# Mixture-of-experts stage: residual parts of the weights two pieces per instruction, one-instruction results, and later transposes of the next rows

## The chip, the cores and the metric

One core of a Trainium2 chip runs the whole layer in one launch. The metric is the device time of that launch in microseconds (us); lower is better. The engines are TensorE (PE, with its weight loads as PEld), VectorE (DVE), ScalarE (ACT), GpSimd (POOL) and SyncE (SP, which only starts transfers here).

## The reference, cut to what matters

The layer is attention followed by a mixture of experts: 1024 tokens, width 1024, 32 experts, four experts per token. Only the experts are touched by the change. Cut, for the rows that an expert receives:

```python
hcat = xb @ w_in[e] + b_in[e]                       # 1024 -> 2048
x_glu = jnp.minimum(hcat[:, :D_FF], 7.0)
x_lin = jnp.clip(hcat[:, D_FF:], -7.0, 7.0)
act = x_glu * jax.nn.sigmoid(1.702 * x_glu) * (x_lin + 1)
y = act @ w_out[e] + b_out[e]                       # 1024 -> 1024
# y times the row's gate is added to the row's token
```

All in float32.

## The kernel before

The experts' stage (`stage_e`) goes through experts one by one, in an order that is written out by hand; the order of the calls is the order on every engine. Expert `e` first multiplies up to 128 gathered rows by `w_in[e]` into `H` (PSUM, four banks), in 16 **input pieces** `i` (`in_mm`): a piece is 128 rows by 1024 columns of the weights. After these, PE works on the 8 **output pieces** `k` of the expert before (`out_mm(e - 1, k)`), which multiply its activations by `w_out`. Between pieces stand other steps, at places that a few constants set: `COLS`, `KB`, `KAB`, `ACI`, `RI`, `LB`.

A float32 product is made of three fast ones (`mm3`, lines 87 to 89). The weight piece is split into a high part `wh` (ACT copies it into the type `F32R`, line 1131) and a low part `wl` (DVE subtracts `wh` from the raw weights, line 1132); the three products are high by high, low by high, high by low, for two halves of 512 columns, six matmuls a piece. `wh` and `wl` are rings of `NW` = 5 tiles. `split_ahead(1)` stands behind each piece and issues the split of the piece five places later, which has to wait until PE has finished the piece that frees its tile.

The steps that the change touches or moves past:

- `columns(e + 1, g)`, three groups g = 0, 1, 2: four transposes of the next expert's rows on PE (line 1119) into a buffer of the PSUM tag `r`, then an ACT copy (line 1122 or 1125) and, for g = 0 and 1, a DVE subtraction (line 1123, `xt`). They stand behind output pieces `COLS` = (1, 3, 4).
- `ring()`: the tag `r` has two buffers, used in turn by everything that asks: `L[e]` (two buffers, set to zero by ACT behind input piece 11), the three groups of `columns`, one blank buffer behind output piece `KB` = 5, and three groups of `act_cols` among the input pieces of the next round. Whoever asks waits until the last reader of the buffer two requests earlier is done.
- `act_a`, `act_l`, `act_b`: the activation. `act_a` (DVE lines 1195, 1197, ACT line 1196) and `act_l` (DVE lines 1204 and 1205 twice each, ACT line 1206) stand behind the input pieces. `act_l` reads the two buffers of `L[e]`.
- `left_in`, `left_out`: an expert's rows beyond 128, under a branch. Without such rows PE jumps over them.
- `result(e - 2)`: behind input piece 1, DVE scales the outputs by gate and modulation into `o` (line 1272, two halves) and `ol` (line 1276), and POOL adds them to the tokens with scattered transfers (lines 1278, 1283).

Of the kernel before, what the change touches and what calls it, by code (L numbers as in the profile page):

```python
# [9 lines left out]
F32 = mybir.dt.float32  # L10
F32R = mybir.dt.float32r
# [3 lines left out]
AF = mybir.ActivationFunctionType  # L15
OP = mybir.AluOpType
# [4 lines left out]
D = 1024  # L21
# [27 lines left out]
class K:  # L49
# [30 lines left out]
    def split(self, hi, lo, src):  # L80

        self.nc.scalar.activation(hi, src, AF.Copy)
        self.nc.vector.tensor_sub(lo, src, hi.bitcast(F32))
# [929 lines left out]
    def stage_e(self):  # L1013
        nc, I, tc = self.nc, self.I, self.tc
# [3 lines left out]
        with ExitStack() as ctx:  # L1018
            sp = self.pool("e1", ctx=ctx)
            ps = self.pool("eps", space=PSUM, ctx=ctx)  # L1020
            ctx.enter_context(tc.manual_schedule())
            RAW_IN, RAW_OUT, XG, XT, ACT, H, L, Y, HL = {}, {}, {}, {}, {}, {}, {}, {}, {}
            VAL = {}

            nrin = [len(self.first) - 2]
            NW = 5

            def rin():
                nrin[0] += 1
# [65 lines left out]
            def sel(e, q, n=128):  # L1095
                return self.selm[:, q, e:e + 1].to_broadcast([128, n])
# [28 lines left out]
                    nc.scalar.activation(xc, p3, AF.Copy)  # L1125
                    XG.pop(e)

            def split_w(src):
                h = sp.tile([128, 1024], F32R, name="wh", tag="wh", bufs=NW)
                l = sp.tile([128, 1024], F32R, name="wl", tag="wl", bufs=NW)  # L1130
                nc.scalar.activation(h, src, AF.Copy)  # L1131
                nc.vector.tensor_tensor(l, src, h.bitcast(F32), op=OP.subtract)  # L1132
                return h, l

            def in_split(e, i):
                k, h = divmod(i, 2)
                HL["in", e, i] = split_w(RAW_IN[e][k][:, 1024 * h:1024 * h + 1024])

            def out_split(e, k):
                HL["out", e, k] = split_w(RAW_OUT[e][k // 2][:, 1024 * (k % 2):1024 * (k % 2) + 1024])  # L1140

            def in_mm(e, i):
                k, h = divmod(i, 2)
# [13 lines left out]
            def beyond(e, unit):  # L1157

                with tc.If(VAL[e] > 128):
                    unit(0)  # L1160
                    with tc.If(VAL[e] > 160):
                        unit(1)
# [24 lines left out]
                beyond(e, unit)  # L1187

            A, AL = {}, {}
            COLS, KB, ACI, RI, LB, KAB = (1, 3, 4), 5, (3, 5, 7), 1, 11, 6  # L1190

            def act_a(e):
                gm = sp.tile([128, D], F32, name="ga", tag="ga", bufs=1)
# [40 lines left out]

            def out_mm(e, k):
                if k == 0:
                    Y[e] = [ps.tile([128, 512], F32, name="y", tag="y", bufs=2) for _ in range(2)]
                    for b in range(2):
                        nc.tensor.matmul(Y[e][b], sel(e, 1), self.bias[:, 512 + 512 * b:1024 + 512 * b],
                                         start=True, stop=False)  # L1240
                wh, wl = HL.pop(("out", e, k))
                ah, al, _ = ACT[e]
                for b in range(2):
                    c = slice(512 * b, 512 * b + 512)
                    self.mm3(Y[e][b], ah[:, k, :], al[:, k, :], wh[:, c], wl[:, c], False, k == 7)

            def left_out(e):
                ac = ACT[e][2]
                p = Y[e][2]

                def unit(u):
                    for j in range(4):
                        nc.tensor.matmul(p[32 * j:32 * j + 32, 256 * u:256 * u + 256],
                                         sel(e, 1, 32).bitcast(F32),
                                         self.bias[:, 512 + 256 * j:768 + 256 * j].bitcast(F32),
                                         start=True, stop=False, tile_position=(0, 32 * j))
                    for k in range(8):
                        jj, h = divmod(k, 2)
                        for j in range(4):
                            nc.tensor.matmul(p[32 * j:32 * j + 32, 256 * u:256 * u + 256],  # L1260
                                             ac[:, 2 * u + h, 32 * jj:32 * jj + 32],
                                             RAW_OUT[e][k // 2][:, 1024 * (k % 2) + 256 * j:1024 * (k % 2) + 256 * j + 256],
                                             start=False, stop=k == 7, tile_position=(0, 32 * j))

                beyond(e, unit)

            def result(e):
                y0, y1, yl = Y.pop(e)
                o = sp.tile([128, D], F32, name="o", tag="o", bufs=1)
                for b, y in enumerate((y0, y1)):  # L1270
                    c = slice(512 * b, 512 * b + 512)
                    nc.vector.scalar_tensor_tensor(o[:, c], y, self.gm[:, e:e + 1], self.gt2[:, c],  # L1272
                                                   op0=OP.mult, op1=OP.mult)
                ol = sp.tile([128, 2, 256], F32, name="ol", tag="ol", bufs=1)
                for u in range(2):
                    nc.vector.scalar_tensor_tensor(ol[:, u], yl[:, 256 * u:256 * u + 256], self.gl[:, u, e:e + 1],
                                                   self.gt2l, op0=OP.mult, op1=OP.mult)
                sc = [nc.gpsimd.indirect_dma_start(  # L1278
                    out=self.acc[:, :], out_offset=bass.IndirectOffsetOnAxis(ap=self.im[:, e:e + 1], axis=0),
                    in_=o, in_offset=None, compute_op=OP.add)]  # L1280
                for u in range(2):
                    nc.gpsimd.memset(spacer, 0.0)
                    i = nc.gpsimd.indirect_dma_start(  # L1283
                        out=self.acc.rearrange("t (j d) -> (t j) d", j=4),
                        out_offset=bass.IndirectOffsetOnAxis(ap=self.il[:, u, e:e + 1], axis=0),
                        in_=ol[:, u, :], in_offset=None, compute_op=OP.add)
                    for x in sc:
                        tc.declare_no_dep(i.ins, x.ins, reason="an expert's tokens are distinct, and so are the dummies")
                    sc.append(i)
# [18 lines left out]
            def split_ahead(used=0):  # L1308

                done[1] += used  # L1310
                while done[0] < min(len(seq), done[1] + NW):
                    kind, e, i = seq[done[0]]
                    if e not in (RAW_IN if kind == "in" else RAW_OUT):
                        break
                    (in_split if kind == "in" else out_split)(e, i)
                    done[0] += 1

            columns(0, 0)
# [2 lines left out]
            for e in range(NE + 1):  # L1321
                if 0 < e < NE - 1:
                    gather(e + 1)
                for i in range(16 if e < NE else 0):
                    in_mm(e, i)
                    if e > 0 or i < 13:
                        split_ahead(1)
                    else:
                        done[1] += 1
                    if i == RI and e > 1:  # L1330
                        result(e - 2)
                    if i in ACI and e > 0:
                        act_cols(e - 1, ACI.index(i))
                    if i == 0 and e == 0:
                        LLS = left_lists()
                    if i == 2 and e == 0:
                        left_lists2(*LLS)
                        gather_left(0)
                        load_out(0, range(2, 4), nc.gpsimd)
                    if i in (9, 10) and e == 0:  # L1340
                        columns(1, i - 9)
                    if i == 11 and e == 0:
                        columns(0, 2)
                        gather_left(1)
                    if i == LB:
                        L[e] = [blank(), blank()]
                if e == NE:
                    result(e - 2)
# [14 lines left out]
                for k in range(8 if e > 0 else 0):  # L1363
                    out_mm(e - 1, k)
                    split_ahead(1)
                    if e < NE:
                        if k in COLS and e + 1 < NE:
                            columns(e + 1, COLS.index(k))
                        if k == (KAB if e < NE - 1 else 3):
                            act_b(e)  # L1370
                        if e == NE - 1 and k in (5, 6, 7):
                            act_cols(e, (5, 6, 7).index(k))
                    if k == KB:
                        Y[e - 1].append(blank())
                if e == 0:
                    act_b(e)
                if e > 0:
                    left_out(e - 1)
                    if e < NE:
                        if e < NE - 1:  # L1380
                            load_out(e)
                        split_ahead()
# [168 lines left out]
```

## Time and profile before

| | |
|---|---|
| median of 3 runs | 2448.65 us (2445.6 to 2449.65) |
| the profiled execution | 2445.95 us |
| its span, first to last instruction | 2444.2 us |
| mean granted TensorE clock | 0.977 of full speed |
| PE, DVE, ACT busy | 93%, 79%, 62% of the span |

The profiled execution stands 2.7 us below the median of the runs. Its span leaves 1.75 us around it. The experts take about the last three fifths of the span, from 937 us on. In the traces a wait in brackets is the idle time of the engine ahead of an instruction, with the instruction that ended it; matmul ends are modelled, so a gap between matmuls is best read from start to start.

### The profile page before, as it was taken

Reading aid. Unit: us, or ns where it says so; the run is one execution under the profiler, and the core shown is the slowest. Engines: PE = TensorE matmul, PEld = TensorE weight load, DVE = VectorE, ACT = ScalarE, POOL = GpSimd, SP = SyncE. Lnnn points to the kernel's source line nnn. Section 1 sums busy time; section 2 is a strip of 40 time slices with the busy share of each in tenths; the row PEclk is TensorE's granted clock in tenths of the full one; section 3 lists DMA queues with packets and bytes.
Section 4 is the critical chain, followed back from the end, with each engine's and each line's share of the span. In section 5 each row is a group of like instructions: output and inputs, shape, how many; then the busy total and the mean of one; then the engine's idle time right before and its main releaser. Section 6 shows DMA issues by size and latency. Waiting matters only on the chain. (4 is left out here: it accounts for less than half of the span.)

```text
span 2444.2 us, 36800 instructions
## 1 busy us (share of the span) xinstructions
PE 2275.3 (93%) x13516; PEld 1760.8 (72%) x13516; DVE 1938.9 (79%) x3051; ACT 1505.0 (62%) x2285; POOL 549.3 (22%) x699
## 2 busy tenths in 40 slices
PE   6999999999999997989999999999999999999993
PEld 3787777787888775767667777767767777777762
DVE  5897087777998677988768898778878978887884
ACT  4321077777888324767656776666767766766762
POOL 2402100000344433122112222112212212222211
PEclk9999999999999997999999999999999999999996
DMA  7546141111110646889778898879779779787875
GB/s 266 182 142 198 48 141 36 35 27 44 30 24 18 231 162 241 326 339 330 263 265 334 306 350 316 292 266 370 279 279 384 285 296 355 281 321 299 311 272 173
DMA packets 133890, 557.00 MB, mean 228 GB/s; under 512 B 18720, under 2 KB 29632, under 8 KB 100880
## 3 DMA queue, kind: packets, MB, share of 16 engines
q1 hardware_dynamic: 103472, 476.21, 51.0%
q0 software_dynamic: 30176, 77.43, 11.4%
q8 instruction: 169, 2.77, 0.5%
q14 instruction: 73, 0.60, 0.1%
HBM read 495.04 MB, written 50.14 MB: 223 GB/s over the span
## 5 line engine op out<-in xcount | busy, mean ns | idle before, releaser
L1131 ACT ACTIVATE wh<-rin 128x1024 fp32r<-128x1024 f32 x520 | 550.3, 1060 | 251.4 <-PE H L89 218.8
L1132 DVE TENSOR_TENSOR wl<-rin,wh 128x1024 fp32r<-128x1024 f32 x520 | 619.4, 1219 | 102.2 <-ACT wh L1131 100.8
L87 PE MATMUL H<-wh,xt 128*128 128x512 f32 x1024 | 414.1, 404 | 0.6 <-issue 0.5
L88 PE MATMUL H<-wl,xt 128*128 128x512 f32 x1024 | 405.5, 396 | 0.6 <-DVE wl L1132 0.6
L89 PE MATMUL H<-wh,xt 128*128 128x512 f32 x1024 | 405.2, 396 | 0.0
L1132 DVE TENSOR_TENSOR wl<-rout,wh 128x1024 fp32r<-128x1024 f32 x248 | 296.5, 1222 | 88.4 <-ACT wh L1131 84.6
L1131 ACT ACTIVATE wh<-rout 128x1024 fp32r<-128x1024 f32 x248 | 256.7, 1054 | 47.1 <-PE H L89 27.2
L89 PEld LDWEIGHTS H<-wh,xt 128*128 128x128 f32 x1024 | 193.5, 189 | 45.7
L87 PEld LDWEIGHTS H<-wh,xt 128*128 128x128 f32 x1024 | 193.9, 189 | 43.5 <-issue 1.4
L88 PEld LDWEIGHTS H<-wl,xt 128*128 128x128 f32 x1024 | 194.0, 189 | 42.7 <-DVE wl L1132 1.0
L87 PE MATMUL y<-wh,at 128*128 128x512 f32 x512 | 210.8, 412 | 0.0
L88 PE MATMUL y<-wl,at 128*128 128x512 f32 x512 | 203.2, 397 | 0.5 <-DVE wl L1132 0.5
L89 PE MATMUL y<-wh,at 128*128 128x512 f32 x512 | 203.4, 397 | 0.0
L1060 POOL DMA_INDIRECT xg<-h2d,im x31 | 33.5, 1081 | 658.8 <-PE r L1119 658.2
L622 ACT ACTIVATE PT<-T 128x512 f32<-128x512 f32 (+1 forms) x256 | 140.8, 577 | 54.4 <-PE T L621 51.9
L1283 POOL DMA_INDIRECT acc<-ol,il x64 | 151.3, 2364 | 17.0 <-DVE wl L1132 15.2
L621 PE MATMUL T<-ident,P 128*128 128x128 f32 x960 | 149.6, 279 | 3.3 <-DVE m L547 2.7
L557 ACT ACTIVATE P<-S,m 128x1024 f32<-128x1024 f32 x128 | 142.9, 1117 | 13.8 <-DVE m L545 7.2
L1278 POOL DMA_INDIRECT acc<-o,im x32 | 51.7, 1615 | 409.0 <-DVE o L1272 377.0
L88 PE MATMUL g<-wl,hh 128*128 128x512 f32 (+1 forms) x368 | 138.0, 375 | 4.1 <-POOL wl L232 4.1
L87 PE MATMUL g<-wh,hh 128*128 128x512 f32 (+1 forms) x368 | 139.1, 378 | 1.1 <-ACT wh L231 0.6
L89 PE MATMUL g<-wh,xl 128*128 128x512 f32 (+1 forms) x368 | 137.3, 373 | 0.0
(338 smaller groups left out, 4376.4 us busy)
## 6 DMA issues: line engine op xcount, KB each, us to landing
rin<-in_w_in SPq DMA_DIRECT2D x252, 1024.0 KB
rout<-in_w_out SPq DMA_DIRECT2D x122, 1024.0 KB
ld<-in_w_ada SPq DMA_DIRECT2D x48, 512.0 KB
wr<-in_w_qkv SPq DMA_DIRECT2D x32, 256.0 KB
Q<-Q SPq DMA_DIRECT2D x32, 256.0 KB
xl<-in_x SPq DMA_DIRECT2D x8, 512.0 KB
xr<-in_x SPq DMA_DIRECT2D x8, 512.0 KB
acc<-x POOLq DMA_DIRECT2D x8, 512.0 KB, 5.5
```

The costliest lines, as they stand in the source:

```text
L87: nc.tensor.matmul(p, ah, bh, start=start, stop=False)
L88: nc.tensor.matmul(p, ah, bl, start=False, stop=False)
L89: nc.tensor.matmul(p, al, bh, start=False, stop=stop)
L557: nc.scalar.activation(parts[k][0], parts[k][1], AF.Exp, bias=m, scale=0.125, accum_out=l2[:, k:k + 1])
L621: nc.tensor.transpose(p[:, k, :], P[:, 128 * j:128 * j + 128], self.ident)
L622: nc.scalar.activation(PT[u - 1][:, 4 * g:4 * g + len(w), :], p[:, :len(w)], AF.Copy)
L1060: nc.gpsimd.indirect_dma_start(out=xg, out_offset=None, in_=self.h2d[:, :], in_offset=bass.IndirectOffsetOnAxis(ap=self.im[:, e:e + 1], ax ...
L1131: nc.scalar.activation(h, src, AF.Copy)
L1132: nc.vector.tensor_tensor(l, src, h.bitcast(F32), op=OP.subtract)
L1278: sc = [nc.gpsimd.indirect_dma_start(out=self.acc[:, :], out_offset=bass.IndirectOffsetOnAxis(ap=self.im[:, e:e + 1], axis=0), in_=o, in_o ...
L1283: i = nc.gpsimd.indirect_dma_start(out=self.acc.rearrange("t (j d) -> (t j) d", j=4), out_offset=bass.IndirectOffsetOnAxis(ap=self.il[:, u ...
```

## The change

It does five things, all in `stage_e`.

1. The rings have `NW` = 6 places instead of 5, and are one tile each, `WH` and `WL`, of six pieces.
2. A split is still one ACT instruction per piece. On DVE an even piece (first half of a raw weight tile) gets no instruction; the odd piece's instruction subtracts both halves, 2048 columns at once.
3. The groups of `columns` stand behind output pieces 3, 4, 5 instead of 1, 3, 4, and the blank buffer behind piece 6 instead of 5.
4. The output `y` is one PSUM tile of 1024 columns instead of two of 512, and `result` reads it with one DVE instruction.
5. The tiles `o` and `ol` take the buffers of `ln` and `lnl`, the linear half of the activation, instead of buffers of their own.

```diff
-            NW = 5
+            NW = 6
...
-            def split_w(src):
-                h = sp.tile([128, 1024], F32R, name="wh", tag="wh", bufs=NW)
-                l = sp.tile([128, 1024], F32R, name="wl", tag="wl", bufs=NW)
-                nc.scalar.activation(h, src, AF.Copy)
-                nc.vector.tensor_tensor(l, src, h.bitcast(F32), op=OP.subtract)
-                return h, l
...
+            WH = sp.tile([128, NW, 1024], F32R, name="wh")
+            WL = sp.tile([128, NW, 1024], F32R, name="wl")
+            npiece = [0]
+
+            def split(kind, e, i):
+                w = (RAW_IN if kind == "in" else RAW_OUT)[e][i // 2]
+                s, h = npiece[0] % NW, i % 2
+                npiece[0] += 1
+                nc.scalar.activation(WH[:, s], w[:, 1024 * h:1024 * h + 1024], AF.Copy)
+                if h:
+                    nc.vector.tensor_tensor(WL[:, s - 1:s + 1], w.rearrange("p (a b) -> p a b", a=2),
+                                            WH[:, s - 1:s + 1].bitcast(F32), op=OP.subtract)
+                HL[kind, e, i] = WH[:, s], WL[:, s]
...
-            COLS, KB, ACI, RI, LB, KAB = (1, 3, 4), 5, (3, 5, 7), 1, 11, 6
+            COLS, KB, ACI, RI, LB, KAB = (3, 4, 5), 6, (3, 5, 7), 1, 11, 6
...
-                    Y[e] = [ps.tile([128, 512], F32, name="y", tag="y", bufs=2) for _ in range(2)]
+                    y = ps.tile([128, 1024], F32, name="y", tag="y", bufs=1)
+                    Y[e] = [y[:, :512], y[:, 512:], y]
...
-                y0, y1, yl = Y.pop(e)
-                o = sp.tile([128, D], F32, name="o", tag="o", bufs=1)
-                for b, y in enumerate((y0, y1)):
-                    c = slice(512 * b, 512 * b + 512)
-                    nc.vector.scalar_tensor_tensor(o[:, c], y, self.gm[:, e:e + 1], self.gt2[:, c],
-                                                   op0=OP.mult, op1=OP.mult)
-                ol = sp.tile([128, 2, 256], F32, name="ol", tag="ol", bufs=1)
+                y, yl = Y.pop(e)[2:]
+                o = sp.tile([128, D], F32, name="o", tag="ln", bufs=1)
+                nc.vector.scalar_tensor_tensor(o, y, self.gm[:, e:e + 1], self.gt2, op0=OP.mult, op1=OP.mult)
+                ol = sp.tile([128, 2, 256], F32, name="ol", tag="lnl", bufs=1)
```

The first place is on DVE, behind `act_l` of the eleventh expert (e = 10), while PE works on the output pieces of the expert before. `rout` are raw tiles of `w_out`, `rin` those of the next expert's `w_in`, `xt` the subtraction of a group of `columns`. Before:

```order
L1205 TENSOR_SCALAR lnl_15609<-r_15454 128x256
L1132 TENSOR_TENSOR wl_15626<-rout_15285,wh_15625 128x1024
L1132 TENSOR_TENSOR wl_15636<-rout_15287,wh_15635 128x1024
L1123 TENSOR_TENSOR xt_15639<-r_15641,xt_15639 128x512
L1132 TENSOR_TENSOR wl_15655<-rout_15287,wh_15654 128x1024
L1132 TENSOR_TENSOR wl_15665<-rin_15592,wh_15664 128x1024
L1123 TENSOR_TENSOR xt_15639<-r_15668,xt_15639 128x512
```

And of the change:

```order
L1206 TENSOR_SCALAR lnl_14962<-r_14817 128x256
L1139 TENSOR_TENSOR wl_10241<-rout_14681,wh_10240 128x2048
L1139 TENSOR_TENSOR wl_10241<-rin_14945,wh_10240 128x2048
L1123 TENSOR_TENSOR xt_15001<-r_15003,xt_15001 128x512
L1123 TENSOR_TENSOR xt_15001<-r_15017,xt_15001 128x512
L1139 TENSOR_TENSOR wl_10241<-rin_14947,wh_10240 128x2048
```

Before, the first `xt` stands behind two splits of output pieces (5 and 6), and the second behind two more. Now both stand behind two instructions of 2048 columns: output pieces 6 and 7, and input pieces 0 and 1 of the next expert.

The second place is on ACT in the same stretch, from the last instruction of `act_l`. Before:

```order
L1206 ACTIVATE gal_15608<-gal_15608 128x512
L1131 ACTIVATE wh_15625<-rout_15285 128x1024
L1131 ACTIVATE wh_15635<-rout_15287 128x1024
L1122 ACTIVATE xt_15639<-r_15641 128x512
L1131 ACTIVATE wh_15654<-rout_15287 128x1024
L1131 ACTIVATE wh_15664<-rin_15592 128x1024
L1122 ACTIVATE xt_15639<-r_15668 128x512
```

And of the change:

```order
L1207 ACTIVATE gal_14961<-gal_14961 128x512
L1137 ACTIVATE wh_10240<-rout_14681 128x1024 x2
L1137 ACTIVATE wh_10240<-rin_14945 128x1024 x2
L1122 ACTIVATE xt_15001<-r_15003 128x512
L1137 ACTIVATE wh_10240<-rin_14947 128x1024
L1122 ACTIVATE xt_15001<-r_15017 128x512
```

Before, the copy of the first group (`xt`, line 1122) has two weight copies between it and `act_l`, now it has four, since the group stands two pieces later in the order.

## Rows read from the trace of the kernel before

**Rows 1.** The page, part 1: busy us (share of the span) and instructions.

```profile
PE 2275.3 (93%) x13516; PEld 1760.8 (72%) x13516; DVE 1938.9 (79%) x3051; ACT 1505.0 (62%) x2285; POOL 549.3 (22%) x699
```

**Rows 2.** Waits of PE, 500 to 2430 us: us in total, times, longest us.

```profile
PE r L1119 <- issue: 26.2, 15, 1.8
PE H L1148 <- PEq L1159: 9.3, 5, 3.2
...
PE H L88 <- DVE wl L1132: 0.6, 1, 0.6
```

**Rows 3.** Timeline, PE, eleventh expert: start, us, instruction, [idle before].

```profile
1413.43 0.39 PE L89 MATMUL y<-wh,at 128*128 128x512 f32 x1
...
1414.83 0.40 PE L89 MATMUL y<-wh,at 128*128 128x512 f32 x1
...
1416.97 0.63 PE L1119 MATMUL r<-ident,xg 128*128 128x128 f32 x4 [1.75 <-issue]
...
1417.36 0.47 PE L87 MATMUL y<-wh,at 128*128 128x512 f32 x1
```

**Rows 4.** Timeline, DVE, the same stretch and one expert later.

```profile
1410.24 3.70 DVE L1132 TENSOR_TENSOR wl<-rout,wh 128x1024 fp32r<-128x1024 f32 x3
1413.86 1.22 DVE L1195 TENSOR_SCALAR ga<-H 128x1024 f32<-128x1024 f32 x1
1415.00 1.21 DVE L1197 TENSOR_SCALAR ln<-H 128x1024 f32<-128x1024 f32 x1
...
1416.46 0.41 DVE L1205 TENSOR_SCALAR lnl<-r 128x256 f32<-128x256 f32 x1
...
1418.85 2.36 DVE L1132 TENSOR_TENSOR wl<-rout,wh 128x1024 fp32r<-128x1024 f32 x2 [1.32 <-ACT wh L1131]
1421.13 0.68 DVE L1123 TENSOR_TENSOR xt<-r,xt 128x512 fp32r<-128x512 f32 x1
...
1455.25 1.21 DVE L1197 TENSOR_SCALAR ln<-H 128x1024 f32<-128x1024 f32 x1
```

**Rows 5.** Timeline, ACT, the same stretch.

```profile
1411.63 1.06 ACT L1131 ACTIVATE wh<-rout 128x1024 fp32r<-128x1024 f32 x1 [0.34 <-PE H L89]
...
1417.24 0.63 ACT L1206 ACTIVATE gal<-gal 128x512 f32<-128x512 f32 x1 [1.07 <-DVE gal L1204]
1417.77 2.00 ACT L1131 ACTIVATE wh<-rout 128x1024 fp32r<-128x1024 f32 x2
1419.67 0.58 ACT L1122 ACTIVATE xt<-r 128x512 fp32r<-128x512 f32 x1
```

**Rows 6.** Groups by line, 500 to 2430 us: busy, mean ns.

```profile
L1132 DVE TENSOR_TENSOR wl<-rin,wh 128x1024 fp32r<-128x1024 f32 x520 | 619.4, 1219 | 102.2 <-ACT wh L1131 100.8
...
L1183 PE MATMUL r<-rin,xc 128*32 128x512 f32 x896 | 99.0, 592 | 0.0
...
L1212 DVE SCALAR_TENSOR_TENSOR gal<-lnl,gal 128x512 f32<-128x512 f32 x32 | 21.9, 683 | 0.0
```

**Rows 7.** Timeline, PE, around two longer idle stretches.

```profile
1100.73 1.19 PE L1148 MATMUL H<-bias,selm 128*128 128x512 f32 x2 [2.65 <-PEq L1159]
1101.72 0.63 PE L87 MATMUL H<-wh,xt 128*128 128x512 f32 x1
...
1684.32 1.19 PE L1239 MATMUL y<-bias,selm 128*128 128x512 f32 x2 [2.36 <-PEq L1159]
```

**Rows 8.** Windows, PE: us, PE busy (count), PEclk, DMA share, GB/s.

```profile
1100.00:1110.00 10.00, 9.27 (x36) 0.83 1.02 405
```

**Rows 9.** Timeline, PE and ACT, an expert with rows beyond 128.

```profile
1225.49 0.60 PE L1119 MATMUL r<-ident,xg 128*128 128x128 f32 x4
...
1228.95 1.06 ACT L1131 ACTIVATE wh<-rin 128x1024 fp32r<-128x1024 f32 x1 [0.30 <-PE y L89]
```

**Rows 10.** Timeline of POOL, and tile ol: its transfers' landing.

```profile
1439.44 2.54 POOL L1283 DMA_INDIRECT acc<-ol,il  x1 [0.26 <-DVE wl L1132]
...
DMA to landing us min/median/max: 4.2/9.5/11.1
```

More of the change, by code (lines that the diff above doesn't have):

```diff
@@ L1126, in columns @@
                     XG.pop(e)
-            def split_w(src):
-                h = sp.tile([128, 1024], F32R, name="wh", tag="wh", bufs=NW)
-                l = sp.tile([128, 1024], F32R, name="wl", tag="wl", bufs=NW)
-                nc.scalar.activation(h, src, AF.Copy)
-                nc.vector.tensor_tensor(l, src, h.bitcast(F32), op=OP.subtract)
-                return h, l
[L1135 to L1140, printed above, removed]
+            WH = sp.tile([128, NW, 1024], F32R, name="wh")
[10 more added lines that the diff above has]
+                HL[kind, e, i] = WH[:, s], WL[:, s]
             def in_mm(e, i):
@@ L1248, in left_out @@
                 ac = ACT[e][2]
-                p = Y[e][2]
+                p = Y[e][3]
                 def unit(u):
@@ L1314, in split_ahead @@
                         break
-                    (in_split if kind == "in" else out_split)(e, i)
+                    split(kind, e, i)
                     done[0] += 1
```

## The prediction

> **What bounds the kernel now.** I read the busy shares first: PE 93%, DVE 79%, ACT 62% [rows 1]. PE is nearly full, so the question is what PE waits for in the experts' stage. The view of PE's waits answers: for weights it waited once, 0.6 us; its largest wait is ahead of the transposes of line 1119, 26.2 us in 15 waits of up to 1.8 us, ended by nothing that the profile names [rows 2]. The timeline of the eleventh expert shows one: the last matmul of output piece 1 starts at 1414.83, the next could follow 0.23 later (six matmuls take 1413.43 to 1414.83, 1.40 us a piece), but the transposes start at 1416.97, so 1.91 us are lost [rows 3]. On DVE the first buffer of `L` gets its last reader, line 1205, from 1416.46 to 1416.87, 0.10 us before PE goes on [rows 4]. So the first group waits for its PSUM buffer, which `act_l` holds. This happens where PE jumps over `left_in`: line 1183's 896 records are 14 groups of 64 [rows 6], and the timeline gives two of these to one expert, so 13 experts have rows beyond 128. The first expert and the last don't have the step in this form; 17 of the other 30 experts jump. In two of the 17 a slow jump on PE had already used up the wait.
>
> **The change part by part.** *Moving the first group* to output piece 3 gives PE two more pieces, 2.80 us, before it asks for that buffer. Against that stands a later DVE, and then the third group. I lay out the eleventh expert anew.
>
> DVE. With six places, the split that waits for the last input piece is that of output piece 5 instead of 4; ACT still makes it at 1411.63 to 1412.69 [rows 5]. Behind it DVE now does 2048 columns. Its price isn't in the trace: 512 columns take 0.683 us and 1024 take 1.219 [rows 6], 0.536 for 512 more, so 2048 take 0.683 + 3 x 0.536 = 2.29 us. Two back to back, from 1418.85 to the next start at 1421.13, take 1.14 each, 0.08 under their duration [rows 4], so the pair holds DVE 2.21 us. The lower bound for the price is 2.0 (no fixed part, 2 x 1.0), the upper 2.44 (no saving at all). The pair ends its hold at 1412.74 + 2.21 = 1414.95, where `act_a` began at 1413.86 before [rows 4]: everything of the activation comes 1.09 us later. The first buffer is free at 1416.87 + 1.09 = 1417.96, and the group may start at 1418.07.
>
> PE. Piece 3 ends at 1415.06 + 2.80 = 1417.86. It waits 0.2 us instead of 1.91: the old wait is nearly gone. The group takes 0.39 [rows 3], piece 4 1.40, the second group 0.39, piece 5 1.40: PE reaches the third group at about 1421.65.
>
> ACT. Its `act_l` instruction started at 1417.24 and the next weight copy at 1417.77; two copies took until 1419.67, 0.95 each [rows 5]. Now 1.09 later: copies of output pieces 6 and 7 and of input pieces 0 and 1 at 1418.86, 1419.81, 1420.76 and 1421.71, all with free places by then, and only then the copy of the first group, 1422.66 to 1423.24.
>
> DVE again. The pair of output pieces 6 and 7 can start when the second copy ends, 1420.9, and holds DVE until 1423.1; the pair of input pieces 0 and 1 until 1425.3; then the first group's subtraction, 0.68 [rows 4], ends at 1426.0. That subtraction is the last reader of the buffer that the third group asks for, since the tag has two. So PE waits from 1421.65 to about 1426.05, **4.4 us**. Before, the subtraction ended at 1421.13 + 0.68 = 1421.81 [rows 4], about when PE got there. The wait moved from the first group to the third and grew: 4.4 + 0.2 - 1.91 = 2.7 us.
>
> For the 17: new waits 17 x 4.6 = 78 us; removed 15 x 1.91 = 29 us; net **+50**. Three pairs stand in this chain, so with a price of 2.0 or 2.44 it ends 0.9 earlier or 0.45 later: +35 to +58.
>
> *Experts with rows beyond 128* (13). There `act_l` is done before output piece 0 ends, and ACT waits for PE's pieces (0.30 us ahead of a copy) [rows 9]; the chain starts from PE. Group 1 came at 1225.49, when piece 1 ended [rows 9]. Piece 3 now ends 2.8 later, 1228.3, and frees the place of input piece 1: ACT copies it from 1228.55 to 1229.6, the pair runs until 1231.9, the subtraction until 1232.6. PE is at the third group after piece 3 + 0.39 + 1.40 + 0.39 + 1.40 = 1231.9. It waits 0.7; the later blank buffer may add 0.1 ahead of `left_out`. 13 x 0.8 = **+10** (bounds 0 and 15).
>
> *Start and end.* The first `wl` of the stage needs two copies and a pair instead of one of each: 1.06 + 2.29 - 1.22, 2.1 us. With the last expert's `act_b` behind pairs I take **+3** (bounds 0 and 8).
>
> *TensorE's clock.* After an idle stretch of 2.65 us matmuls take 0.63 instead of 0.40 us [rows 3, 7]; the window's mean granted clock is 0.83 [rows 8], that is 3.4 of 10 us at 1.2 instead of 2.4 GHz, 1.7 us of work lost. The stretch of 2.36 us shows the same matmuls of 1.19 [rows 7]; the 15 waits of 1.75 don't [rows 3]. A wait of 4.4 us is longer than any of these, so I expect falls. How much of the slow stretch lies inside the wait itself isn't seen: 0 to 1.7 us for each of 17. I take 1.2, nearer to the upper row: **+20** (0 to 29).
>
> *Parts at nothing.* A pair saves DVE 2 x 1.219 - 2.29 = 0.15 us, twelve times an expert, and `result` saves some too. DVE isn't what PE waits for outside this place: PE waited 0.6 us for a `wl` [rows 2], and DVE itself waited 102.2 us ahead of line 1132, nearly all for ACT [rows 6]. With a pair done some 3.5 us after the second copy starts and six places of 1.40 us, weights stay ahead. `o` and `ol` in the buffers of `ln` and `lnl` add waits of DVE for the scattered transfers, ahead of `act_a` and `act_l`, with the whole chain above queued behind. The last transfer was issued at 1439.44 and lands within 11.1 us, by 1450.5; line 1197 comes at 1455.25 [rows 4, 10]. Both move about a microsecond; 4 us of cover remain. Without it each microsecond would be paid by up to 30 experts. The transfers of weights wait for branches that PE passes, and a slower PE gives them more room. POOL's gathers wait for later transposes, but fetch rows a whole expert ahead (some 40 us).
>
> The Trainium skill, Perfetto Trace Analysis, section Optimizing Scalar/DVE Operations, has two rules here. Larger operations can raise throughput if the engine is saturated; by that the twelve pairs would give 30 x 12 x 0.15 = 54 us. But where an engine isn't saturated and still makes others idle, smaller instructions, which finish sooner, may help; by that the pairs give nothing and the chain above stays. DVE's waits for ACT say that the second applies.
>
> **The sum.** 50 + 10 + 3 + 20 = +83 us. On the profiled execution's 2445.95 that is 2529; on the median of the runs, 2448.65, it is **2531**.
>
> **The rivals.**
> - *The wait is there but the clock holds.* For it: the falls of rows 7 followed branches, none a buffer. Against: both stretches of rows 7 are shorter than this wait, and the clock fell. 2448.65 + 63 = 2512.
> - *The third group hardly waits: faster.* This is the change doing what its places suggest: the first buffer freed in time, and no new wait. It would give 17 x 0.2 - 29 = -26, with the start 2426. It decides at the third group: the first group's subtraction must end by 1421.65, 4.4 us sooner than laid out, which is just the two pairs (2 x 2.21) that the order puts ahead of it. An engine that took the subtraction ahead of them would do it; in all rows of DVE that I read, instructions run in the order of the program, and the copy on ACT alone, at 1422.66, is too late.
> - *DVE bounds after all*: then its 54 us less of work show in the time, 2395. Against: it stood idle for ACT [rows 6] and PE hardly for it [rows 2]. This is the first of the skill's two rules above.
> - *The wait is there but short*, 1 to 2.5 us, if ACT and DVE make up more of their delay than my lay-out gives: net 17 x (1.75 + 0.2) - 29 + 13 = +17, about 2466, and no clock falls.
> - *The scattered transfers come too late for `ln`*: on top of the sum 2 us in each of 30 experts would give 2591. It needs landings of 15 us, none above 11.1 is seen [rows 10].
>
> **How the numbers follow.** Forecast with clock falls 0.60, clock holding 0.20, short wait 0.09, no wait 0.07, DVE as the bound 0.01, late transfers 0.03. The likeliest case alone spans 2501 (+35, 0, 0, +17) to 2550 (+58, +15, +8, +20). For 8 in 10 the range takes in the clock's holding, with its low end at 2448.65 + 35 = 2484, and the upper end of the forecast: 2482 to 2552. Measurements of this kernel differ by up to 0.17% within three runs, so 0.2% (5 us) is about what can be told from no change. Faster 0.08; same 0.02, a part of the short wait; slower 0.90.
>
> **What would show it.** Right: in PE's waits the third group (transposes of `xgl`) waits some 4.4 us in 17 experts, ended by the subtraction of `xt`; waits of 1.75 us ahead of the first group fall to a few tenths; the pair takes 2.29 us; the mean granted clock falls below 0.977, with some 3.4 us at the lower level behind such waits; PE's total waits grow by about 60 us. Wrong: no idle time ahead of the `xgl` transposes, or the subtraction of the first group before the pair of input pieces 0 and 1 in time; then the gain of about 25 us would stand.

## The result and the profile after

| | before | changed |
|---|---|---|
| median of 4 runs each | 2447.12 us (2444.24 to 2449.65) | 2521.49 us (2518.6 to 2525.74) |
| ratio, 95% interval | | 1.0306 (1.0286 to 1.0326) |
| the profiled execution / its span | 2445.95 / 2444.2 us | 2520.61 / 2518.8 us |
| mean granted TensorE clock | 0.977 | 0.961 |

The change makes the kernel 74.4 us slower; the spans of the two profiled executions differ by 74.6. The forecast was 2531 (+83), range 2482 to 2552.

First the busy times on the page (part 1, busy us, share and instructions), beside [rows 1]:

```profile
PE 2299.8 (91%) x13516; PEld 1782.6 (71%) x13516; DVE 1901.4 (75%) x2635; ACT 1506.7 (60%) x2285; POOL 590.9 (23%) x699
```

DVE has 416 instructions and 37.5 us less to do, and nothing comes of it. PE runs the same 13516 instructions and is busy 24.5 us longer: the same matmuls took longer, and the granted clock fell from 0.977 to 0.961. The other 50 us are idle time. PE's waits, 500 to 2510 us (us in total, times, longest us), beside [rows 2]:

```profile
PE r L1119 <- DVE xt L1123: 74.7, 31, 4.1
PE H L1149 <- PEq L1160: 9.2, 4, 3.8
PE r L1227 <- DVE ga L1212: 6.5, 2, 6.0
...
PE H L88 <- DVE wl L1139: 2.5, 1, 2.5
```

The groups by line split line 1119 into the first two groups (`xg`) and the third (`xgl`); the last part of a row is the idle time ahead. The changed kernel:

```profile
L1119 PE MATMUL r<-ident,xg 128*128 128x128 f32 x256 | 39.5, 278 | 1.8 <-PE y L89 0.9 <-issue 0.3
...
L1119 PE MATMUL r<-ident,xgl 128*128 128x128 f32 x128 | 26.4, 341 | 78.0 <-DVE xt L1123 74.7 <-DVE lnl L1206 3.3
```

And the same two rows of the kernel before:

```profile
L1119 PE MATMUL r<-ident,xg 128*128 128x128 f32 x256 | 39.6, 279 | 26.8 <-issue 26.2 <-PE y L89 0.3 <-DVE gmain L854 0.3
...
L1119 PE MATMUL r<-ident,xgl 128*128 128x128 f32 x128 | 19.6, 276 | 3.3 <-DVE lnl L1205 3.3
```

The wait did not go away; it moved from the first group (26.8 to 1.8 us) to the third (3.3 to 78.0 us). The eleventh expert shows how, in the timeline of PE (start, us, instruction, [idle before]):

```profile
1436.91 0.39 PE L89 MATMUL y<-wh,at 128*128 128x512 f32 x1
1437.37 0.63 PE L1119 MATMUL r<-ident,xg 128*128 128x128 f32 x4
...
1440.83 0.40 PE L89 MATMUL y<-wh,at 128*128 128x512 f32 x1
1445.34 1.11 PE L1119 MATMUL r<-ident,xgl 128*128 128x128 f32 x4 [4.12 <-DVE xt L1123]
1446.11 0.77 PE L87 MATMUL y<-wh,at 128*128 128x512 f32 x1
1446.68 0.63 PE L88 MATMUL y<-wl,at 128*128 128x512 f32 x1
```

of DVE:

```profile
1436.85 0.42 DVE L1206 TENSOR_SCALAR lnl<-r 128x256 f32<-128x256 f32 x1
...
1440.19 2.29 DVE L1139 TENSOR_TENSOR wl<-rout,wh 128x2048 fp32r<-128x2048 f32 x1 [2.26 <-ACT wh L1137]
1442.40 2.28 DVE L1139 TENSOR_TENSOR wl<-rin,wh 128x2048 fp32r<-128x2048 f32 x1
1444.60 1.28 DVE L1123 TENSOR_TENSOR xt<-r,xt 128x512 fp32r<-128x512 f32 x2
```

and of ACT:

```profile
1438.17 1.99 ACT L1137 ACTIVATE wh<-rout 128x1024 fp32r<-128x1024 f32 x2
1440.06 1.99 ACT L1137 ACTIVATE wh<-rin 128x1024 fp32r<-128x1024 f32 x2
1441.96 0.58 ACT L1122 ACTIVATE xt<-r 128x512 fp32r<-128x512 f32 x1
```

The first group follows piece 3 after 0.46 us from start to start, 0.23 more than from one matmul to the next, where 1.91 us were lost before [rows 3]. Its copy on ACT ends at 1442.54, but its subtraction on DVE starts only at 1444.60, behind the two pairs that stand ahead of it in the order, and PE waits for it from 1441.06 to 1445.34, 4.28 us from start to start. Behind it matmuls start 0.43 us apart instead of 0.23. Windows of 5 us behind this wait and behind one that began at 1726 us (us, PE busy (count), PEclk, DMA share, GB/s):

```profile
1445.30:1450.30 5.00, 4.96 (x14) 0.50 1.03 419
1729.10:1734.10 5.00, 4.99 (x20) 0.66 1.02 421
```

0.50 is the lower level throughout; in the second window a part of the time is at the full clock. The timeline has 17 such waits, 15 of them of 4.06 to 4.13 us and two (from 1726 and 2256 us) of 3.1, where a slow jump over a branch stood ahead. Slow matmuls follow all 17. The other 14 of the 31 waits in the row above are of 0.48 us each: 13 in the experts with rows beyond 128, and one at 964 us, early in the stage.

### The profile page after: what moved, and what is told of

Same layout as the page of the kernel before. It is cut to its first block, busy times and chain, and to the rows that moved or that the text cites. A ratio compares the mean times of both kernels' runs of the same rounds, so it can differ in the third digit from the quotient of the medians.

```text
span 2518.8 us, 36232 instructions
## 1 busy us (share of the span) xinstructions
PE 2299.8 (91%) x13516; PEld 1782.6 (71%) x13516; DVE 1901.4 (75%) x2635; ACT 1506.7 (60%) x2285; POOL 590.9 (23%) x699
## 3 DMA queue, kind: packets, MB, share of 16 engines
q1 hardware_dynamic: 103472, 476.21, 49.7%
## 5 line engine op out<-in xcount | busy, mean ns | idle before, releaser
L1139 DVE TENSOR_TENSOR wl<-rin,wh 128x2048 fp32r<-128x2048 f32 x260 | 594.3, 2287 | 182.9 <-ACT wh L1137 182.8
L1139 DVE TENSOR_TENSOR wl<-rout,wh 128x2048 fp32r<-128x2048 f32 x124 | 284.3, 2293 | 130.1 <-ACT wh L1137 130.1
L87 PE MATMUL y<-wh,at 128*128 128x512 f32 x512 | 222.0, 434 | 0.0
L88 PE MATMUL y<-wl,at 128*128 128x512 f32 x512 | 210.9, 412 | 0.0
L89 PE MATMUL y<-wh,at 128*128 128x512 f32 x512 | 210.8, 412 | 0.0
L1060 POOL DMA_INDIRECT xg<-h2d,im x31 | 43.4, 1399 | 636.4 <-PE r L1119 635.8
L1068 POOL DMA_INDIRECT xgl<-h2d,il x64 | 125.1, 1955 | 131.5 <-PE r L1119 101.1
```

The source lines that it names most:

```text
L87: nc.tensor.matmul(p, ah, bh, start=start, stop=False)
L88: nc.tensor.matmul(p, ah, bl, start=False, stop=False)
L89: nc.tensor.matmul(p, al, bh, start=False, stop=stop)
L1060: nc.gpsimd.indirect_dma_start(out=xg, out_offset=None, in_=self.h2d[:, :], in_offset=bass.IndirectOffsetOnAxis(ap=self.im[:, e:e + 1], ax ...
L1068: nc.gpsimd.indirect_dma_start(out=xl[:, u, :], out_offset=None, in_=self.h2d.rearrange("t (j d) -> (t j) d", j=4), in_offset=bass.Indirec ...
L1139: nc.vector.tensor_tensor(WL[:, s - 1:s + 1], w.rearrange("p (a b) -> p a b", a=2), WH[:, s - 1:s + 1].bitcast(F32), op=OP.subtract)
```

## The experiments

The theory after the result: in an expert whose branch is jumped, the third group has to wait for the first group's PSUM buffer, whose last reader DVE takes behind two pairs of weight subtractions; the lower clock comes on top. Rivals: the later places alone or the longer instructions alone explain it; shared buffers or the ring tiles cost something; the longer busy time is not the idle time's doing. All were timed against the kernel before on the same chip. "Groups 1, 2" and "group 3" are PE's idle us ahead of their transposes, including 3.3 us ahead of one transpose near 970 us in every kernel.

| kernel | median us | ratio to before | groups 1, 2 | group 3 |
|---|---|---|---|---|
| before | 2447 to 2449 | 1 | 26.8 | 3.3 |
| changed | 2521.49 | 1.0306 (1.0286 to 1.0326) | 1.8 | 78.0 |
| e1_places | 2470.72 | 1.0091 (1.0060 to 1.0122) | 0.3 | 43.7 |
| e2_pairs | 2480.68 | 1.0143 (1.0112 to 1.0175) | 49.8 | 7.4 |
| e3_rest | 2446.97 | 0.9999 (0.9989 to 1.0009) | 30.8 | 3.3 |
| e4_order | 2465.32 | 1.0076 (1.0051 to 1.0100) | 2.2 | 32.6 |
| e5_bank | 2451.92 | 1.0014 (1.0004 to 1.0023) | 1.8 | 3.8 |
| e6_fill | 2499.81 | 1.0214 (1.0199 to 1.0230) | 2.2 | 12.9 |
| e9_places_234 | 2475.12 | 1.0111 (1.0091 to 1.0130) | 5.5 | 37.0 |
| e7_third_apart | 2430.77 | 0.9927 (0.9914 to 0.9941) | 5.0 | 3.3 |
| e8_all_apart | 2547.39 | 1.0395 (1.0380 to 1.0409) | 93.1 | 3.6 |
| e10_order_old | 2442.17 | 0.9974 (0.9962 to 0.9986) | 5.0 | 3.3 |

### The change taken apart: places, pairs, the rest

**e1_places**: the kernel before with the new places only.

```diff
-            COLS, KB, ACI, RI, LB, KAB = (1, 3, 4), 5, (3, 5, 7), 1, 11, 6
+            COLS, KB, ACI, RI, LB, KAB = (3, 4, 5), 6, (3, 5, 7), 1, 11, 6
```

> The kernel before with only the places changed: groups of transposes behind output pieces 3, 4, 5, blank buffer behind 6; five places, one subtraction per piece. Theory (the first group's subtraction is late, and the third group waits for its PSUM buffer): the activation is not delayed, so the first group does not wait; four copies and four subtractions of 1.14 us stand ahead of the first group's subtraction, which ends near 1424.1 in the eleventh expert's time while PE is there at 1421.45: a wait of about 2.7 us in 17 experts, 46 against 29 removed, +17 us, and some falls of the clock, in all +17 to +40. Rival (only the 2048-column instructions hurt, the places are good): the 29 us are gained, -25 us.

Measured +24 us. In PE's waits the same wait has appeared, shorter:

```profile
PE r L1119 <- DVE xt L1123: 40.4, 17, 2.5
```

The places alone move the wait to the third group; they give no gain.

**e2_pairs**: the changed kernel with the places of before, so the pairs and all the rest, but not the move.

```diff
-            COLS, KB, ACI, RI, LB, KAB = (3, 4, 5), 6, (3, 5, 7), 1, 11, 6
+            COLS, KB, ACI, RI, LB, KAB = (1, 3, 4), 5, (3, 5, 7), 1, 11, 6
```

> The changed kernel with the old places 1, 3, 4 and 5; pairs, six places, one-instruction results and shared buffers stay. Theory: the pair of output pieces 4 and 5 makes the activation 1.09 us later, so the first group waits 3.0 instead of 1.9 us in 17 experts, and the third 0.8: 65 against 29 before, +36 us, and falls of the clock after 3.0 us, in all +35 to +60. Rival (the new places alone make the loss, pairs save DVE work): 0 to -10 us.

Measured +34 us. The wait stays ahead of the first group and grows from 1.75 to about 3 us, since the pair delays the activation that frees the buffer. In the eleventh expert `act_a` on DVE starts 3.30 us after the start of ACT's last weight copy ahead of it, in the kernel before 2.23; so it comes 1.07 us later:

```profile
PE r L1119 <- DVE lnl L1206: 52.8, 18, 3.3
```

**e3_rest**: the changed kernel with the old places and one subtraction of 1024 columns per piece; the ring tiles with six places, the one-instruction result and the shared buffers stay.

```diff
-                if h:
-                    nc.vector.tensor_tensor(WL[:, s - 1:s + 1], w.rearrange("p (a b) -> p a b", a=2),
-                                            WH[:, s - 1:s + 1].bitcast(F32), op=OP.subtract)
+                nc.vector.tensor_tensor(WL[:, s], w[:, 1024 * h:1024 * h + 1024], WH[:, s].bitcast(F32), op=OP.subtract)
...
-            COLS, KB, ACI, RI, LB, KAB = (3, 4, 5), 6, (3, 5, 7), 1, 11, 6
+            COLS, KB, ACI, RI, LB, KAB = (1, 3, 4), 5, (3, 5, 7), 1, 11, 6
```

> The changed kernel with the old places and one subtraction of 1024 columns per piece: what is left are six places in one tile, one-instruction results, and o and ol in the buffers of ln and lnl. Theory: nothing of this is on the path, within 5 us of before, waits of 1.75 us ahead of the first group as before. Rival (the shared buffers make the activation wait for the scattered transfers, or the one-tile ring adds waits): a good part of the 74 us, +20 or more.

Measured 2446.97 us, ratio 0.9999 (0.9989 to 1.0009): these parts together cost and give nothing that can be measured. So the loss is the places' and the pairs': 24 and 34 us alone, 74 together, more than their sum of 58.

### The order, the buffer, the clock

**e4_order**: the changed kernel, but a group of `columns` is asked for ahead of `split_ahead(1)` behind the same piece, so one split fewer stands ahead of each copy and subtraction.

```diff
                     out_mm(e - 1, k)
+                    if e < NE and k in COLS and e + 1 < NE:
+                        columns(e + 1, COLS.index(k))
                     split_ahead(1)
                     if e < NE:
-                        if k in COLS and e + 1 < NE:
-                            columns(e + 1, COLS.index(k))
```

> The changed kernel with each group of transposes ahead of the split that follows the same output piece, not behind it. Theory: on ACT three copies instead of four, on DVE one pair instead of two stand ahead of the first group's subtraction, which then ends near 1423.8; PE is at the third group at 1421.65, so the wait falls from 4.3 to about 2.2 us, is gone in the 13 experts with rows beyond 128, and the clock falls hardly or not: 17 x 2.4 - 29 + 3, +15 us, at most +30. Rival (weights come late behind the long instructions, whatever stands in the order): near the changed kernel, +60 to +75.

Measured +18 us instead of the changed kernel's +74. The third group's wait falls from 4.12 to 1.92 us; the difference of 2.20 is what one pair holds DVE (starts at 1440.19, 1442.40 and 1444.60 above). Slow matmuls still follow 10 of the 15 waits, where hardly a fall of the clock was expected.

```profile
PE r L1119 <- DVE xt L1123: 29.3, 16, 1.9
```

So the pairs that stand ahead of the subtraction in the order make the wait: with one of the two gone from there, 56 of the 74 us are gone.

**e5_bank**: the changed kernel, but the third group doesn't ask the ring; it is written into the fourth bank of the next expert's `H`, which the activation has freed by then.

```diff
-                p = ring()
+                if g == 2 and e > 1:
+                    H[e] = ps.tile([128, 2048], F32, name="H", tag="H", bufs=1)
+                    p = H[e][:, 1536:2048]
+                else:
+                    p = ring()
...
-                if i == 0:
+                if i == 0 and e not in H:
```

> The changed kernel with one difference: the third group of transposes writes into the fourth PSUM bank of the next expert's H, which is free by then, and no longer asks for a buffer of the tag r. DVE and ACT keep their order and are as late as before. Theory (the wait is for the buffer): the waits of 4.1 us ahead of the third group are gone. What is late next is the low part of output piece 6, which the pair delivers at about 1423.2 in the eleventh expert's time, while PE asks at 1422.3: 1 us in 17 experts; the buffers of the tag come round one request earlier and may cost 1 to 2 us in some others. In all -5 to +25 us against before, no falls of the clock there. Rival (PE would wait anyway, for low parts that come as late as the subtraction): PE waits some 4 us at output piece 6 instead, near +74.

Measured +2.6 us. With all subtractions still behind the pairs, the wait ahead of the third group is gone but for the two experts that still use the ring, and some 72 us of the 74 with it. By line, as above:

```profile
L1123 PE MATMUL H<-ident,xgl 128*128 128x128 f32 x120 | 18.0, 272 | 0.0
L1123 PE MATMUL r<-ident,xgl 128*128 128x128 f32 x8 | 1.3, 283 | 3.8 <-DVE lnl L1210 3.3 <-DVE xt L1127 0.5
```

What is late next are smaller things:

```profile
PE r L1259 <- ACT r L1104: 12.0, 12, 1.6
PE y L88 <- DVE wl L1143: 9.7, 15, 0.7
```

The first is `left_out`, which asks for the ring in the experts with rows beyond 128; the second are weights that the pairs give later.

**e6_fill**: the changed kernel with 17 more matmuls ahead of the third group in the 17 experts that jump. They write a bank of the next expert's `H`, which is written anew later, so they change no output.

```diff
-                if i == 0:
+                if i == 0 and e not in H:
...
+                        if k == COLS[2] and e in (1, 2, 3, 4, 8, 9, 10, 11, 14, 16, 18, 20, 21, 24, 25, 27, 29):
+                            H[e + 1] = ps.tile([128, 2048], F32, name="H", tag="H", bufs=1)
+                            for _ in range(17):
+                                nc.tensor.matmul(H[e + 1][:, :512], sel(e, 1), self.bias[:, 512:1024],
+                                                 start=True, stop=True)
```

> The changed kernel, in which PE fills its long wait: in the 17 experts that jump over left_in, 17 extra matmuls (bias by selection, 0.23 us each, 4.0 us in all) into the next expert's H, which is written anew later, stand ahead of the third group. The chain on ACT and DVE is the same, so the third group starts when it did. Theory (20 of the 74 us are matmuls at 1.2 GHz behind the waits): PE stays busy, the clock does not fall there, some 15 to 25 us less than the changed kernel, about +52 against before. Rival (the clock's falls lie inside the waits and cost nothing, all 74 us are waits): as the changed kernel, +74, or more by what the extra matmuls overrun.

The fill takes the place of the idle time, and the third group comes 4.28 us late as before:

```profile
1438.45 0.40 PE L89 MATMUL y<-wh,at 128*128 128x512 f32 x1
1438.68 4.09 PE L1369 MATMUL H<-bias,selm 128*128 128x512 f32 x17
1442.96 0.66 PE L1119 MATMUL r<-ident,xgl 128*128 128x128 f32 x4 [0.19 <-DVE xt L1123]
1443.38 0.48 PE L87 MATMUL y<-wh,at 128*128 128x512 f32 x1
```

The granted clock of the stage (windows as above), in the changed kernel:

```profile
1000.00:2430.00 1430.00, 1325.58 (x7237) 0.97 0.80 298
```

and with the fill:

```profile
1000.00:2410.00 1410.00, 1365.88 (x7542) 1.00 0.81 301
```

The time is 2499.81 us, 1.0214 (1.0199 to 1.0230). PE does 289 matmuls more, and yet the kernel is faster than the changed one by 1.0306 - 1.0214 = 0.0092, some 22 us (by the two intervals 16 to 29), which is the clock's part. The timelines agree: from 937 us on, the matmuls of `mm3` that take 0.58 us or more number 31 before, 142 in the changed kernel and 32 with the fill. 120 of the 142 stand behind the 17 waits; at 0.43 instead of 0.23 us from start to start they cost 24 us. The remaining 50 us stay although PE isn't idle there: they are the lateness itself.

### Could the idea of the change pay?

**e7_third_apart**: the kernel before, with the edit of e5_bank (shown there) and the groups behind pieces 2, 3 and 4.

```diff
...
-            COLS, KB, ACI, RI, LB, KAB = (1, 3, 4), 5, (3, 5, 7), 1, 11, 6
+            COLS, KB, ACI, RI, LB, KAB = (2, 3, 4), 4, (3, 5, 7), 1, 11, 6
```

> A version for both: the kernel before (five places, 1024-column subtractions) with the third group in the fourth bank of the next expert's H, groups behind output pieces 2, 3, 4, blank buffer behind 4. Theory: PE reaches the first group at 1416.46 instead of 1415.06, its buffer is free at 1416.97, so 0.5 instead of 1.91 us in 17 experts, and no other wait takes its place, since only two groups ask the tag for buffers: 15 x 1.4 us, about -20, -12 to -25. Rival (the ring of buffers is needed by others too, the wait moves on to the activation's transposes): 0 to -8.

Measured 2430.77 us, 18.6 below the kernel before and faster than both. None of the waits for the subtraction is left:

```profile
PE r L1123 <- PE y L89: 4.6, 13, 0.4
```

The Trainium skill, Perfetto Trace Analysis, section Optimization Strategy, says that the same gap, repeated on the engine that should be full, can mean that SBUF or PSUM lacks room for the next tile. The traces agree: 15 equal waits of 1.75 us before, and with one bank more and the new places 13 of at most 0.4 us.

**e9_places_234**: the kernel before with those places, but all three groups in the ring.

```diff
-            COLS, KB, ACI, RI, LB, KAB = (1, 3, 4), 5, (3, 5, 7), 1, 11, 6
+            COLS, KB, ACI, RI, LB, KAB = (2, 3, 4), 4, (3, 5, 7), 1, 11, 6
```

> The kernel before with the places 2, 3, 4 and the blank buffer behind 4, all groups in the tag r: the version with the third group apart without its bank. Theory: the first group waits 0.5 us; three copies and three subtractions stand ahead of the first group's subtraction, which ends near 1422.95 in the eleventh expert's time, while PE asks for the third group's buffer at 1420.55: 2.4 us in 17 experts, 17 x 2.9 - 29 = +20 us, with falls of the clock up to +35. Rival (the gain with the third group apart came from the places, not from the bank): -12 to -20 us.

Measured +27 us, with 33.7 us of waits ahead of the third group. The gain of e7_third_apart needs the bank.

**e8_all_apart**: as e7_third_apart, but all three groups in banks 2 to 4 of the next `H`.

```diff
-                p = ring()
+                if e > 1:
+                    if g == 0:
+                        H[e] = ps.tile([128, 2048], F32, name="H", tag="H", bufs=1)
+                    p = H[e][:, 512 + 512 * g:1024 + 512 * g]
+                else:
+                    p = ring()
...
```

> As the one with the third group apart, but all three groups write into the second to fourth banks of the next expert's H, so none asks the tag r. Theory: the first group waits for act_a alone, which reads H until 1416.2, before PE is there at 1416.46: no wait is left, 15 x 1.75 us, about -24, -15 to -28; the activation's transposes may wait for the reader of the blank buffer where rows beyond 128 are, 1 us in some. Rival (the two buffers of the tag come round sooner and the waits move to the activation's transposes in most experts): -10 or less.

Measured 2547.39 us, 1.0395 (1.0380 to 1.0409): +98 where a gain was expected. Now the second group waits for the subtraction of the first, in all 30 experts, although they use different banks (4.3 to 4.6 us in 17 of them, 1.2 in 13):

```profile
PE H L1124 <- DVE xt L1128: 92.8, 30, 4.5
```

The program waits on DVE between two groups of the same tile `H`. Why it holds that wait between banks stays open. The miss fits the theory in so far as the same subtraction, awaited one group earlier, makes PE wait longer: 4.5 us, against 2.2 in e9_places_234.

**e10_order_old**: the kernel before with the order of e4_order (shown there) and the groups behind 2, 4 and 5.

```diff
-            COLS, KB, ACI, RI, LB, KAB = (1, 3, 4), 5, (3, 5, 7), 1, 11, 6
+            COLS, KB, ACI, RI, LB, KAB = (2, 4, 5), 5, (3, 5, 7), 1, 11, 6
...
```

> The kernel before with the groups behind output pieces 2, 4, 5, each ahead of the split that follows the same piece; no other buffer. Theory: the first group waits 0.5 us; its subtraction stands behind two subtractions as in the kernel before and ends at 1421.8, while PE asks for the third buffer at 1421.95: no wait. 15 x 1.4 us, -12 to -21. Rival (any later place delays the first group's subtraction past the third group): 0 to +20.

Measured 2442.17 us, 0.9974 (0.9962 to 0.9986): a gain of 5.6 us, less than expected. The waits ahead of the groups are gone as meant (4.6 us in 14 small ones), but in its profile more is lost elsewhere: behind the branches 32.8 us against 25.6 before, and in two waits ended by nothing that the profile names 4.2 us against 0.5 in one:

```profile
PE H L1148 <- PEq L1159: 14.9, 6, 4.1
PE H L1148 <- PEq L1161: 7.4, 11, 2.8
PE y L1239 <- PEq L1161: 5.5, 12, 0.5
PE y L1239 <- PEq L1159: 5.0, 5, 2.1
PE r L1119 <- issue: 4.6, 14, 0.4
PE H L87 <- issue: 4.2, 2, 2.3
```

In the profiles of the other ten kernels the rows behind branches add up to 21 to 27 us. The profiled execution, 2445.45 us, is also one of the longer of the 12, which go from 2434.77 to 2449.38. Whether the removed wait comes back there, or these waits merely vary from execution to execution, was not settled.

## Why the prediction came out as it did

The mechanism was right; the sum, 83 against 74, was 9 us too high, chiefly by the waits of the groups.

- **The pair.** Priced at 2.29 us with a hold of 2.21; measured 2.29 and 2.20. The lower bound of 2.0 was looser than its rows: four times 0.536 is 2.14 without a fixed part. The long instruction delays what stands behind it, as laid out (1.07 us in e2_pairs, where 1.09 was forecast): 34 us alone. DVE's saving was put too high, at 54 us: two subtractions back to back take 2.36 us and not 2 x 1.22, so a pair saves 0.07 there, and with the results DVE has 37.5 us less to do. The Trainium skill, Perfetto Trace Analysis, section Optimizing Scalar/DVE Operations, has the rule on smaller instructions that the prediction weighed against the one on larger ones. It is the one that held: with less to do on DVE e2_pairs loses 34 us, and e3_rest without the pairs loses nothing.
- **First group.** 0.2 us left of 1.91; measured 0.23 from start to start.
- **Third group.** 4.4 us; measured 4.28. Order and durations of ACT and DVE came as laid out; e4_order and e5_bank show that the pairs and the buffer make it. But two of the 17 waits were shorter, 3.1 us of idle time: a slow jump had already used up part, as in two of the old waits, and the prediction counted those for the old wait alone. From start to start the 17 experts lose 45 us more, where 50 were forecast.
- **Experts with rows beyond 128.** 0.8 us each; measured 0.65 from start to start (0.48 of idle time), and 1.3 us in all ahead of `left_out`, 0.1 each. This term held.
- **Idle time ahead of the groups together.** The rows by line give (1.8 + 78.0) - (26.8 + 3.3) = 49.7 us, where the sum had 50 + 10 = 60. About half of the difference is the measure: the sum went from start to start, and by that the two terms come to 45 + 10 = 55. The other half is the two shorter waits and 0.12 us less in each of the 15.
- **Start and end.** 3 us; at the start PE waited 2.5 us for the first `wl` instead of 0.6 [rows 2], so 1.9 (2.1 forecast). The kernel before has a second wait for a `wl`, 0.5 us near its end, where the prediction speaks of one; it is gone. At the end line 1227 waited 6.0 us for the last expert's `act_b`. The same wait was 3.2 us before, so 2.8 where about 1 was meant. Together some 5 us.
- **Clock.** 20 us; by e6_fill 22. The value between the ends of 0 and 29 was chosen and not worked out, so that it came this near is luck in part. The reason given, that a wait longer than 2.36 us brings a fall, also doesn't hold in general (last section).
- **Parts at nothing.** e3_rest: nothing, within 0.1% either way. In the changed kernel's waits of DVE none ahead of `act_a` or `act_l` is ended by a scattered transfer.
- **The sum as measured.** 49.7 + 5 + 22 = 77 us, against 74.6 of the span; the waits behind branches of this execution are 23.4 us, 2.2 less than before.

Of the rivals, the clock's holding fell to the slow matmuls behind all 17 waits and to e6_fill, the short wait and the missing wait to the rows of the third group, DVE as the bound to its falling busy time at a rising total.

## What to carry to other kernels

When two buffers are used in turn, moving the request that waits can hand the wait to the request two places later, as it did here in four kernels; it did not in e10_order_old, where the last reader came earlier too. So find that reader in its engine's order and count the instructions ahead of it; merging those into longer ones made the wait longer here (4.1 instead of 2.5 us) even though the engine had less to do. Look first for a free bank for one request: together with the places 2, 3 and 4, which alone lose 27 us, it gave 18.6 us here with no other work saved.

## What the runs showed of the hardware

The clock did not follow the length of a wait alone. Counting, in the timelines of eight kernels, the waits ahead of a group behind which matmuls at the lower level (0.63 instead of 0.40 us) follow: none of 15 waits of 1.75 us in the kernel before; 3 of 16 of 1.6 to 2.0 us in e3_rest; 10 of 15 of 1.92 us in e4_order; 11 of 15 of 2.2 us in e9_places_234; 8 of 17 of 1.6 to 2.5 us in e1_places; 8 of 16 of 2.8 to 3.1 us in e2_pairs; all 17 of 3.1 to 4.1 us in the changed kernel; in e8_all_apart all 17 of 4.3 to 4.6 us and none of 13 of 1.2 us. Two waits of e4_order, alike but for what followed, in windows of 5 us:

```profile
1050.50:1055.50 5.00, 4.97 (x16) 0.66 1.01 413
1092.50:1097.50 5.00, 3.40 (x16) 1.00 1.01 416
```

Both stand behind 1.9 us of idle time; one shows 0.66, the other 1.00. What decides between them was not tried. And the waits of PE behind a branch, mostly 0.3 to 0.6 us, reach 4.1 us here and there (the longest in e10_order_old), at other experts in other kernels' profiles.
